# First pair of a gated MLP kernel: x loaded, cast and transposed in pieces of 256 tokens by half of K, products ordered by halves of K

## Chip, cores, metric

One core of a Trainium2 chip. The metric is the device time of one execution in microseconds (us), the lower the better. "The profile" is the hardware profile of one execution. Engines: TensorE (PE in the profile), VectorE (DVE), ScalarE (ACT), GpSimd (POOL); SP is the sequencer that issues most transfers.

## The reference

```python
# x (8, 1024, 1024) -> 8192 tokens x K = 1024; w_gate, w_up (1024, 4096); w_down (4096, 1024), all float32
gate = x @ w_gate
up   = x @ w_up
gate = 0.5 * gate * (1 + np.tanh(np.sqrt(2 / np.pi) * (gate + 0.044715 * gate ** 3)))
return (gate * up) @ w_down
```

## The kernel before

The kernel works in eight passes of 1024 tokens, in float16 with fast matrix multiplication schemes. In the first pass, gate and up are made in 16 "pairs" of 256 columns of each weight. All pairs but the first use a Strassen-like scheme: sums of blocks of x and of the weights go in. The first pair is special: its inputs come straight from memory in float32, before anything else can run, so it uses plain products and is written by hand. It loads x (two halves of 512 tokens, `mh`), casts it on VectorE, transposes it on TensorE into PSUM (the memory that TensorE's results go to; the kernel uses eight banks of it), copies it out, and multiplies. `kh` is the half of K, `w` is gate or up, `j` one of two blocks of 128 columns, `MQ` = 256 tokens, `MH` = 512.

```python
    def x0_load(mh, g):                      # 128 tokens, all of K: rows of 4 KB
        r0 = mh * MH + g * P
        nc.sync.dma_start(out=x0_f32[mh][:, g], in_=x2[r0 : r0 + P, :])
    def x0_cast(mh, g):
        nc.vector.tensor_scalar(x0_f16[:, mh * G + g], x0_f32[mh][:, g], XSC, None, MUL)
    def x0_transpose(mh, g, b):              # 8 transposes into PSUM bank b, two copies out
        ...
    # ... in first_pair():
        for g in range(G):
            x0_cast(0, g)
        warm(9)                              # warm-up matmuls of ones
        late = []
        for g in range(G):
            late.append(x0_transpose(0, g, 4 + g))
            warm(2 if g < G - 1 else 3)
        for w in range(2):
            cast_first(w, 0, slice(0, 256))              # ScalarE
        for f in late:
            f()
        for w in range(2):
            cast_first(w, 1, slice(0, 256), nc.vector.tensor_copy)
        for kh in range(2):
            products(0, kh, slice(0, MH))
        # ... second half of tokens: two transposed pieces, 256 tokens of products, two more, the rest
        outputs(0, 0)
        for w in range(2):
            cast_first(w, 0, slice(256, 512))            # the second pair's weights, ScalarE
        nc.gpsimd.tensor_copy(mark, staging0(1, 0)[:, 0, 256:257])   # waits for load 14
        load_raw(0, 1)                                   # then the third and fourth pairs' weights
        ...
        sum_x(1); sum_w(0, 1, 0); sum_w(0, 1, 1); sum_x(2)           # [joined here] sums of the second
        outputs(1, 0); outputs(1, 1)                                 # pair, all on VectorE
        sum_x(3); sum_w(0, 1, 2); sum_w(0, 1, 3); sum_x(4)
    # order of the 16 first loads, 512 KB each: x(0) four, weights four, x(1) four, next weights four
```

In the timelines read here each engine's instructions start in the order in which they are written.

Of the kernel before, what the change touches and what calls it, by code (L numbers as in the profile page):

```python
# [10 lines left out]
FP16 = mybir.dt.float16  # L11
ADD = mybir.AluOpType.add
SUB = mybir.AluOpType.subtract
MUL = mybir.AluOpType.mult
# [5 lines left out]
XSC = 1.0 / 16.0  # L20
# [153 lines left out]
def kernel(  # L174
# [8 lines left out]
    nc = tc.nc  # L183
    x2 = x.flatten_outer_dims()
    out2 = out.flatten_outer_dims()
    P = 128
# [4 lines left out]
    MH = 512  # L191
    MQ = 256
    HH = H // 2
    KH = K // P // 2
# [3 lines left out]
    G = MH // P  # L198
# [20 lines left out]
    identity = const.tile([P, P], FP16, name="identity")  # L219
# [3 lines left out]
    xq = {  # L223
        n: const.tile([P, KH, MH], FP16, name=f"x_{n}") for n in ("b11", "b12", "b21", "b22")
    }
# [13 lines left out]
    ps_all = psum.tile([P, 8, MH], FP32, name="ps")  # L239
# [5 lines left out]
    ps_free = deque(range(8))  # L245
# [16 lines left out]
    def sum_x(n):  # L262
        o, a, b = {
            1: ("t1", "b12", "b11"), 2: ("t2", "b22", "t1"),
            3: ("t3", "b22", "b12"), 4: ("t4", "b21", "t2"),
        }[n]
        nc.vector.tensor_tensor(xq[o], xq[a], xq[b], SUB)
# [8 lines left out]
    def combine(o, op, a, b):  # L276
# [9 lines left out]
    x0_f32 = {  # L286
        mh: hf[n].bitcast(FP32).rearrange("p (t k) -> p t k", t=G)
        for mh, n in ((0, "a11"), (1, "a21"))
    }
    x0_f16 = hf["a12"].rearrange("p (t a) -> p t a", t=2 * G)  # L290

    def x0_load(mh, g):
        r0 = mh * MH + g * P
        nc.sync.dma_start(out=x0_f32[mh][:, g], in_=x2[r0 : r0 + P, :])

    def x0_cast(mh, g):
        nc.vector.tensor_scalar(x0_f16[:, mh * G + g], x0_f32[mh][:, g], XSC, None, MUL)

    def x0_transpose(mh, g, b):
        h = x0_f16[:, mh * G + g]  # L300
        ps = ps_all[:, b].bitcast(FP16).rearrange("p (k m) -> p k m", m=P)
        for k in range(2 * KH):
            nc.tensor.transpose(ps[:, k], h[:, k * P : (k + 1) * P], identity)
        c = slice(g * P, (g + 1) * P)
        nc.vector.tensor_copy(xq["b11" if mh == 0 else "b12"][:, :, c], ps[:, 0:KH])
        if mh:
            nc.scalar.copy(xq["b22"][:, :, c], ps[:, KH : 2 * KH])
        else:
            return lambda: nc.scalar.copy(xq["b21"][:, :, c], ps[:, KH : 2 * KH])


    def raw(p, q):
        o = 8192 * ((q + p) % 2)
        return rg[:, o : o + 8192].rearrange("p (w k n) -> p w k n", w=2, k=2 * KH)
# [6 lines left out]
    def staging0(w, kh):  # L321
        f = hf["a22"] if kh else xc[:, 8192:16384]
        return f[:, w * 4096 : (w + 1) * 4096].bitcast(FP32).rearrange("p (k n) -> p k n", k=KH)

    def load_first(w, kh, cols):
        nc.sync.dma_start(
            out=staging0(w, kh)[:, :, cols], in_=w_v[w][:, kh * KH : (kh + 1) * KH, cols]
        )

    def cast_first(w, kh, cols, copy=nc.scalar.copy):  # L330
        copy(raw(0, 0)[:, w, kh * KH : (kh + 1) * KH, cols], staging0(w, kh)[:, :, cols])

    def load_raw(p, q):
        if q < NQ:
            for w in range(2):
                nc.gpsimd.dma_start(
                    out=raw(p, q)[:, w], in_=w_v[w][:, :, q * 512 : (q + 1) * 512]
                )

    def sum_w(p, i, k):  # L340
        if i >= NP:
            return
        r, s = raw(p, i // 2), ssum(i)
        e = (i % 2) * 2 * P
        a11, a12 = r[:, :, 0:KH, e : e + P], r[:, :, KH : 2 * KH, e : e + P]
        a21, a22 = r[:, :, 0:KH, e + P : e + 2 * P], r[:, :, KH : 2 * KH, e + P : e + 2 * P]
        o, a, b, op = (
            (s[:, 0], a21, a22, ADD), (s[:, 1], s[:, 0], a11, SUB),
            (s[:, 2], a11, a21, SUB), (s[:, 3], a12, s[:, 1], SUB),
        )[k]  # L350
        nc.vector.tensor_tensor(o, a, b, op)  # L351
# [328 lines left out]
    def gate_up_one(p):  # L680
# [9 lines left out]
        for i in range(NP):  # L690
# [6 lines left out]
            if p == 0 and i == 0:  # L697
                first_pair()
                continue
# [490 lines left out]

    def first_pair():
        bank = {(mh, j, w): 4 * mh + 2 * j + w for mh in range(2) for j in range(2) for w in range(2)}

        def products(mh, kh, c):
            for w in range(2):
                for j in range(2):
                    for k in range(KH):
                        nc.tensor.matmul(
                            ps_all[:, bank[mh, j, w], c],
                            raw(0, 0)[:, w, kh * KH + k, j * P : (j + 1) * P],  # L1200
                            xq[f"b{kh + 1}{mh + 1}"][:, k, c],
                            start=(kh == 0 and k == 0 and c.start == 0),
                            stop=(kh == 1 and k == KH - 1),
                            skip_group_check=True,
                        )

        def outputs(mh, j):
            t = tmp_free.popleft()
            g, u = bank[mh, j, 0], bank[mh, j, 1]
            nc.scalar.activation(tmp[:, t], ps_all[:, g], GELU, scale=GSC)  # L1210
            nc.vector.tensor_tensor(
                hq[f"a{mh + 1}{j + 1}"][:, 0, :], ps_all[:, u], tmp[:, t], MUL
            )
            tmp_free.append(t)

        def warm(n):

            for _ in range(n):
                nc.tensor.matmul(ps_all[:, 0], warm_w, warm_x, start=True, stop=True)

        warm_w, warm_x = hf["s3"][:, 0:P], hf["s3"][:, P : P + MH]
        nc.vector.memset(hf["s3"][:, 0 : P + MH], 1.0)
        nc.scalar.activation(mark, hf["s3"][:, 0:1], GELU)
        for g in range(G):
            x0_cast(0, g)
        warm(9)
        late = []
        for g in range(G):
            late.append(x0_transpose(0, g, 4 + g))
            warm(2 if g < G - 1 else 3)  # L1230

        for w in range(2):
            cast_first(w, 0, slice(0, 256))
        for f in late:
            f()
        for w in range(2):
            cast_first(w, 1, slice(0, 256), nc.vector.tensor_copy)
        for kh in range(2):
            products(0, kh, slice(0, MH))
        for g in range(2):  # L1240
            x0_cast(1, g)
        for g in range(2):
            x0_transpose(1, g, 6 + g)
        for g in range(2, G):
            x0_cast(1, g)
        outputs(0, 0)
        for w in range(2):
            cast_first(w, 0, slice(256, 512))

        nc.gpsimd.tensor_copy(mark, staging0(1, 0)[:, 0, 256:257])  # L1250
        load_raw(0, 1)
        for kh in range(2):
            products(1, kh, slice(0, MQ))
        for g in range(2, G):
            x0_transpose(1, g, g - 2)
        outputs(0, 1)
        for w in range(2):
            cast_first(w, 1, slice(256, 512))
        for kh in range(2):
            products(1, kh, slice(MQ, MH))  # L1260

        ps_free.clear()
        ps_free.extend((0, 2, 1, 3, 4, 5, 6, 7))
        sum_x(1)
        sum_w(0, 1, 0)
        sum_w(0, 1, 1)
        sum_x(2)
        outputs(1, 0)
        outputs(1, 1)
        sum_x(3)  # L1270
        sum_w(0, 1, 2)
        sum_w(0, 1, 3)
        sum_x(4)

    for g in range(G):
        x0_load(0, g)
    for c in (slice(0, 256), slice(256, 512)):
        for kh in range(2):
            for w in range(2):
                load_first(w, kh, c)  # L1280
        if c.start == 0:
            for g in range(G):
                x0_load(1, g)
    for p in range(NPASS):
        if p < FAST:
            gate_up_one(p)
# [36 lines left out]
```

## Time and profile before

| | before |
|---|---|
| time, median of the first 6 executions | 2256.32 us (2255.86 to 2257.22) |
| profiled execution: span | 2254.4 us |
| first product of real data | 11.47 us |
| first matmul of the second pair | 28.72 us |
| TensorE waits after 26 us, whole execution | one, 0.4 us, at 279.69 us |

The lines that carry this are in the prediction. A timeline line is: start, length, engine, source line, operation, output<-input, shape, count; in brackets, the idle time before it and what ended it. A line of the waits is: who waited for whom, then us in total, times, longest. A line of the chain is: start, length, what. In these the shown length of a matmul group has a tail of about 0.17 us.

### The profile page before, as it was taken

The page shows a single profiled execution, that of the slowest core. Times are in us where ns is not written, and L with a number is a line of the kernel's source. Part 1 is how long each engine was busy: PE and PEld are TensorE (multiplying, and loading weights), DVE is VectorE, ACT ScalarE, POOL GpSimd, SP SyncE. Part 2 cuts the span into 40 slices and gives each one's busy share as a digit, 9 for nine tenths or more (in the row PEclk, how much of TensorE's full clock was granted, in tenths as well). Part 3 has the DMA queues.
Part 4 walks back from the last instruction along what each step waited for, and adds up shares of the span by engine and source line. Part 5 has one row for each costly group of instructions (what it writes and reads, how often), then busy time and mean ns, then how long its engine had stood idle before and what let it go on. Part 6 is the DMA issues. An engine that isn't in the chain of part 4 may idle for free.

```text
span 2254.4 us, 42805 instructions
## 1 busy us (share of the span) xinstructions
PE 2246.1 (100%) x16634; PEld 1625.6 (72%) x16634; DVE 1561.7 (69%) x2190; ACT 956.1 (42%) x1866; POOL 679.3 (30%) x825
## 2 busy tenths in 40 slices
PE   9999999999999999999999999999999999999999
PEld 4444444444444445888888888888888888888888
DVE  6576458883588755777776677666786667866674
ACT  4444135651355622666125550356404653055520
POOL 1332013330133200555014550255403543044520
PEclk9999999999999999999999999999999999999999
DMA  9898969989999999999998999989999889988876
GB/s 241 163 207 218 284 184 241 263 264 283 255 227 249 282 309 349 328 342 370 302 339 274 317 304 318 322 270 324 311 324 316 285 308 326 311 311 277 289 285 225
DMA packets 308093, 642.46 MB, mean 285 GB/s; under 512 B 79088, under 2 KB 185328, under 8 KB 287344
## 3 DMA queue, kind: packets, MB, share of 16 engines
q1 hardware_dynamic: 253104, 566.57, 73.2%
q0 software_dynamic: 54784, 73.14, 19.3%
q8 instruction: 130, 2.13, 0.4%
q14 instruction: 75, 0.61, 0.1%
HBM read 574.36 MB, written 138.41 MB: 316 GB/s over the span
## 4 chain that ended last, share of the span: by engine, by line
PE 87%; DMA 2%; SPq 0%; DVE 0%; issue 0%; DVEq 0%
PE ps L848 40%; PE ps L1099 20%; PE ps L626 17%; PE ps L991 10%; DMA wd_quads<-x_sums 1%; SPq L255 0%; DMA ring<-wd_ops 0%; DVE x_sums L452 0%; DVE h_a L923 0%; DVE tmp L1168 0%; DVE x_sums L278 0%; SPq L487 0%; DVEq L278 0%; SPq L535 0%
## 5 line engine op out<-in xcount | busy, mean ns | idle before, releaser
L848 PEld LDWEIGHTS <-ring 128*128 128x128 f16 x8320 | 814.1, 98 | 94.4
L825 POOL TENSOR_TENSOR h_a<-tmp 128x256 f16<-128x256 f32 x640 | 469.3, 753 | 839.3 <-ACT tmp L813 831.9
L848 PE MATMUL ps<-x_sums,ring 128*128 128x256 f16 x5760 | 655.8, 273 | 0.0
L810 DVE TENSOR_TENSOR tmp<-tmp,ps 128x512 f32<-128x512 f32 x640 | 414.5, 683 | 148.1 <-PE ps L848 99.7
L626 PEld LDWEIGHTS <-ring 128*128 128x128 f16 x2632 | 257.5, 98 | 310.4
L795 ACT COPY tmp<-ps 128x512 f32<-128x512 f32 x520 | 304.1, 585 | 237.5 <-PE ps L848 162.8
L626 PE MATMUL ps<-x_sums,ring 128*128 128x512 f16 x1504 | 339.8, 379 | 0.0
L813 ACT ACTIVATE tmp<-tmp 128x256 f32<-128x256 f32 x640 | 264.1, 418 | 172.8 <-DVE tmp L808 79.4
L848 PE MATMUL ps<-x_b,ring 128*128 128x256 f16 x2560 | 305.6, 273 | 0.0
L808 DVE TENSOR_TENSOR tmp<-ps,tmp 128x512 f32<-128x512 f32 x240 | 165.4, 689 | 145.2 <-ACT tmp L795 101.0
L626 PE MATMUL ps<-x_b,ring 128*128 128x512 f16 x1128 | 259.1, 379 | 0.0
L652 POOL TENSOR_TENSOR h_a<-tmp 128x512 f16<-128x512 f32 x94 | 144.5, 1537 | 374.8 <-ACT tmp L650 271.9
L1099 PEld LDWEIGHTS <-h_a 128*128 128x128 f16 x2240 | 219.2, 98 | 25.4
L991 PE MATMUL ps<-ring,h_a 128*128 128x512 f16 x1024 | 222.3, 379 | 0.4 <-DMA ring<-wd_ops 0.4
L1099 PE MATMUL ps<-ring,h_a 128*128 128x256 f16 x1920 | 216.1, 273 | 0.0
L991 PEld LDWEIGHTS <-h_a 128*128 128x128 f16 x1152 | 112.7, 98 | 136.6 <-DMA ring<-wd_ops 0.9
L645 DVE TENSOR_TENSOR tmp<-ps,tmp 128x512 f32<-128x512 f32 x188 | 127.2, 683 | 112.6 <-ACT tmp L637 111.1
L1156 ACT ACTIVATE tmp<-ps 128x512 f32<-128x512 f32 x60 | 35.3, 597 | 362.6 <-PE ps L1099 274.6
L1168 DVE SCALAR_TENSOR_TENSOR tmp<-ps,tmp 128x512 f32<-128x512 f32 x120 | 81.1, 690 | 97.5 <-PE ps L1099 66.6
L351 DVE TENSOR_TENSOR ring<-ring 128x1024 f16<-128x1024 f16 x188 | 138.7, 751 | 11.1 <-DMA ring<-in_w_up_dram 6.9
L637 ACT COPY tmp<-ps 128x512 f32<-128x512 f32 x188 | 109.9, 586 | 77.8 <-PE ps L626 77.8
L1099 PE MATMUL ps<-ring,x_sums 128*128 128x256 f16 x1120 | 126.3, 273 | 0.0
(102 smaller groups left out, 1532.0 us busy)
## 6 DMA issues: line engine op xcount, KB each, us to landing
ring<-w_ops SPq DMA_DIRECT2D x480, 512.0 KB, 5.0
ring<-wd_quads SPq DMA_DIRECT2D x110, 1024.0 KB, 7.0
ring<-wd_ops SPq DMA_DIRECT2D x35, 1024.0 KB, 8.2
out_dram<-tmp SPq DMA_DIRECT2D x128, 256.0 KB, 6.6
w_ops<-h_s SPq DMA_DIRECT2D x128, 256.0 KB, 6.7
ring<-in_w_gate_dram POOLq DMA_DIRECT2D x23, 1024.0 KB, 10.5
ring<-in_w_up_dram POOLq DMA_DIRECT2D x23, 1024.0 KB, 17.8
wd_quads<-x_sums SPq DMA_DIRECT2D x131, 128.0 KB, 6.4
```

What stands on the lines that cost most here:

```text
L351: nc.vector.tensor_tensor(o, a, b, op)
L626: nc.tensor.matmul(ps(b, w), lhs[:, k], rhs[:, k, :], start=(first and k == 0), stop=(k == KH - 1), skip_group_check=True,)
L645: nc.vector.tensor_tensor(o, ps("b", w), o, ADD)
L652: nc.gpsimd.tensor_tensor(hq[TO[n]][:, i, :], tmp[:, t[n, 1]], tmp[:, t[n, 0]], MUL)
L795: nc.scalar.copy(tmp[:, t[o[1]]], ps_all[:, bank[o[2]]])
L808: nc.vector.tensor_tensor(d, b, a, SUB)
L810: nc.vector.tensor_tensor(d, a, b, ADD if o[4] == "add" else SUB)
L813: nc.scalar.activation(d, d, GELU, scale=GSC)
L825: nc.gpsimd.tensor_tensor(h, tmp[:, t[o[1]], MQ : 2 * MQ], g, MUL)
L848: nc.tensor.matmul(ps_all[:, bank[c], w * MQ : (w + 1) * MQ], lhs[:, w, k], rhs[:, k], start=(first and w == 0 and k == 0), stop=(k == KH ...
L991: nc.tensor.matmul(ps_all[:, bank[b, g]], lhs[:, j, g * P : (g + 1) * P], dc[:, n, :], start=(first and j == 0), stop=(j == NP - 1), skip_ ...
L1099: nc.tensor.matmul(ps_all[:, bank[c], m * MQ : (m + 1) * MQ], lhs[:, j, m * P : (m + 1) * P], rhs[:, j, :], start=(first and j == 0 and m ...
```

## The change

The intent: start the products sooner. The first product needs only half of K of x and one weight piece, 1.5 MB instead of 2.5. So x comes in pieces of 256 tokens by half of K, the products run over the first half of K for all tokens, and what belongs to the second half of K follows.

```diff
-    def x0_load(mh, g):
-        r0 = mh * MH + g * P
-        nc.sync.dma_start(out=x0_f32[mh][:, g], in_=x2[r0 : r0 + P, :])
+    def x0_load(mh, gp, kh):
+        r0 = mh * MH + gp * MQ
+        nc.sync.dma_start(
+            out=x0_piece(x0_f32[mh], gp, kh),
+            in_=x2[r0 : r0 + MQ, kh * KH * P : (kh + 1) * KH * P].rearrange("(t p) k -> p t k", p=P),
+        )
 ... (x0_cast likewise)
+    def x0_transpose(mh, gp, kh, b, first=nc.vector.tensor_copy):
 ...
+        first(o[:, 0:2], ps[:, 0:2])
+        nc.scalar.copy(o[:, 2:4], ps[:, 2:4])
 ... first_pair():
+        warm(7)
+        for gp in range(2):
+            x0_cast(0, gp, 0)
+        x0_transpose(0, 0, 0, 4, nc.scalar.copy)
+        warm(2)
+        x0_transpose(0, 1, 0, 5)
+        warm(2)
+        cast_first(0, 0, c0, dve, two[0])
+        cast_first(0, 0, c0, nc.scalar.copy, two[1])
+        cast_first(1, 0, c0, dve)
+        product(0, 0, 0, 0)
 ... (three more products; pieces (1,0,0), (1,1,0), (0,0,1), (0,1,1), each cast, transposed, copied)
+        cast_first(1, 1, c0, dve)
+        product(0, 1, 1, 0)
+        x0_cast(1, 0, 1)
+        x0_transpose(1, 0, 1, 7)
+        outputs(0, 0)
+        product(0, 1, 1, 1)
+        for j in range(2):
+            product(1, 1, 0, j, lo)
+        x0_cast(1, 1, 1)
+        x0_transpose(1, 1, 1, 7)
+        outputs(0, 1)
         for w in range(2):
-            cast_first(w, 0, slice(256, 512))
+            cast_first(w, 0, c1)
 ... (mark, load_raw as before; the remaining products)
+        cast_first(0, 1, c1)
+        cast_first(1, 1, c1, dve)
 ... (the sums and outputs(1, ...) as before)
-    for g in range(G):
-        x0_load(0, g)
+    for kh in range(2):
+        for gp in range(2):
+            x0_load(0, gp, kh)
+        for w in range(2):
+            load_first(w, kh, slice(0, 256))
+        for gp in range(2):
+            x0_load(1, gp, kh)
 ... (then the second pair's four weight pieces, as before)
```

More of the change, by code (lines that the diff above doesn't have):

```diff
@@ L290, with x0_piece, x0_cast @@
     x0_f16 = hf["a12"].rearrange("p (t a) -> p t a", t=2 * G)
-    def x0_load(mh, g):
-        r0 = mh * MH + g * P
-        nc.sync.dma_start(out=x0_f32[mh][:, g], in_=x2[r0 : r0 + P, :])
-    def x0_cast(mh, g):
-        nc.vector.tensor_scalar(x0_f16[:, mh * G + g], x0_f32[mh][:, g], XSC, None, MUL)
-    def x0_transpose(mh, g, b):
-        h = x0_f16[:, mh * G + g]
-        ps = ps_all[:, b].bitcast(FP16).rearrange("p (k m) -> p k m", m=P)
-        for k in range(2 * KH):
-            nc.tensor.transpose(ps[:, k], h[:, k * P : (k + 1) * P], identity)
-        c = slice(g * P, (g + 1) * P)
-        nc.vector.tensor_copy(xq["b11" if mh == 0 else "b12"][:, :, c], ps[:, 0:KH])
-        if mh:
-            nc.scalar.copy(xq["b22"][:, :, c], ps[:, KH : 2 * KH])
-        else:
-            return lambda: nc.scalar.copy(xq["b21"][:, :, c], ps[:, KH : 2 * KH])
+    def x0_piece(t, gp, kh):
+        return t[:, 2 * gp : 2 * gp + 2, kh * KH * P : (kh + 1) * KH * P]
+    def x0_load(mh, gp, kh):
[4 more added lines that the diff above has]
+        )
+    def x0_cast(mh, gp, kh):
+        nc.vector.tensor_scalar(
+            x0_piece(x0_f16, 2 * mh + gp, kh), x0_piece(x0_f32[mh], gp, kh), XSC, None, MUL
+        )
+    def x0_transpose(mh, gp, kh, b, first=nc.vector.tensor_copy):
+        h = x0_piece(x0_f16, 2 * mh + gp, kh)
+        ps = ps_all[:, b].bitcast(FP16).rearrange("p (k m) -> p k m", m=MQ)
+        o = xq[f"b{kh + 1}{mh + 1}"][:, :, gp * MQ : (gp + 1) * MQ]
+        for k in range(KH):
+            for t in range(2):
+                nc.tensor.transpose(
+                    ps[:, k, t * P : (t + 1) * P], h[:, t, k * P : (k + 1) * P], identity
+                )
+        first(o[:, 0:2], ps[:, 0:2])
+        nc.scalar.copy(o[:, 2:4], ps[:, 2:4])
     def raw(p, q):
@@ L328, in load_first, with cast_first @@
         )
-    def cast_first(w, kh, cols, copy=nc.scalar.copy):
-        copy(raw(0, 0)[:, w, kh * KH : (kh + 1) * KH, cols], staging0(w, kh)[:, :, cols])
+    def cast_first(w, kh, cols, copy=nc.scalar.copy, ks=slice(0, KH)):
+        o = raw(0, 0)[:, w, kh * KH : (kh + 1) * KH, cols]
+        copy(o[:, ks], staging0(w, kh)[:, ks, cols])
     def load_raw(p, q):
@@ L1192, in first_pair, with product @@
         bank = {(mh, j, w): 4 * mh + 2 * j + w for mh in range(2) for j in range(2) for w in range(2)}
-        def products(mh, kh, c):
-            for w in range(2):
-                for j in range(2):
-                    for k in range(KH):
-                        nc.tensor.matmul(
-                            ps_all[:, bank[mh, j, w], c],
-                            raw(0, 0)[:, w, kh * KH + k, j * P : (j + 1) * P],
-                            xq[f"b{kh + 1}{mh + 1}"][:, k, c],
-                            start=(kh == 0 and k == 0 and c.start == 0),
-                            stop=(kh == 1 and k == KH - 1),
-                            skip_group_check=True,
-                        )
+        full, lo, hi = slice(0, MH), slice(0, MQ), slice(MQ, MH)
+        def product(mh, kh, w, j, c=full):
+            for k in range(KH):
+                nc.tensor.matmul(
+                    ps_all[:, bank[mh, j, w], c],
+                    raw(0, 0)[:, w, kh * KH + k, j * P : (j + 1) * P],
+                    xq[f"b{kh + 1}{mh + 1}"][:, k, c],
+                    start=(kh == 0 and k == 0 and c.start == 0),
+                    stop=(kh == 1 and k == KH - 1),
+                    skip_group_check=True,
+                )
         def outputs(mh, j):
@@ L1223, in first_pair @@
         nc.scalar.activation(mark, hf["s3"][:, 0:1], GELU)
-        for g in range(G):
-            x0_cast(0, g)
-        warm(9)
-        late = []
-        for g in range(G):
-            late.append(x0_transpose(0, g, 4 + g))
-            warm(2 if g < G - 1 else 3)
-        for w in range(2):
-            cast_first(w, 0, slice(0, 256))
-        for f in late:
-            f()
-        for w in range(2):
-            cast_first(w, 1, slice(0, 256), nc.vector.tensor_copy)
-        for kh in range(2):
-            products(0, kh, slice(0, MH))
@@ L1240, in first_pair @@
-        for g in range(2):
-            x0_cast(1, g)
-        for g in range(2):
-            x0_transpose(1, g, 6 + g)
-        for g in range(2, G):
-            x0_cast(1, g)
-        outputs(0, 0)
-        for w in range(2):
-            cast_first(w, 0, slice(256, 512))
+        two, dve = (slice(0, 2), slice(2, 4)), nc.vector.tensor_copy
+        c0, c1 = slice(0, 256), slice(256, 512)
+        warm(7)
+        for gp in range(2):
+            x0_cast(0, gp, 0)
+        x0_transpose(0, 0, 0, 4, nc.scalar.copy)
@@ new lines, in first_pair @@
+        warm(2)
[5 more added lines that the diff above has]
+        product(0, 0, 0, 0)
+        product(0, 0, 0, 1)
+        product(0, 0, 1, 0)
+        x0_cast(1, 0, 0)
+        x0_transpose(1, 0, 0, 6, nc.scalar.copy)
+        product(0, 0, 1, 1)
+        x0_cast(1, 1, 0)
+        x0_transpose(1, 1, 0, 7)
+        product(1, 0, 0, 0, lo)
+        product(1, 0, 0, 0, hi)
@@ new lines, in first_pair @@
+        x0_cast(0, 0, 1)
+        x0_transpose(0, 0, 1, 7)
+        product(1, 0, 0, 1)
+        x0_cast(0, 1, 1)
+        x0_transpose(0, 1, 1, 7)
+        product(1, 0, 1, 0)
+        cast_first(0, 1, c0, dve, two[0])
+        cast_first(0, 1, c0, nc.scalar.copy, two[1])
+        product(0, 1, 0, 0)
+        product(0, 1, 0, 1)
+        cast_first(1, 1, c0, dve)
[4 more added lines that the diff above has]
+        product(0, 1, 1, 1)
@@ L1250, in first_pair @@
+        for j in range(2):
[3 more added lines that the diff above has]
+        outputs(0, 1)
+        for w in range(2):
+            cast_first(w, 0, c1)
         nc.gpsimd.tensor_copy(mark, staging0(1, 0)[:, 0, 256:257])
         load_raw(0, 1)
+        product(1, 1, 1, 0, lo)
+        product(1, 1, 0, 0, hi)
+        product(1, 1, 0, 1, hi)
+        product(1, 1, 1, 0, hi)
         for kh in range(2):
-            products(1, kh, slice(0, MQ))
@@ L1254, in first_pair @@
-        for g in range(2, G):
-            x0_transpose(1, g, g - 2)
-        outputs(0, 1)
-        for w in range(2):
-            cast_first(w, 1, slice(256, 512))
-        for kh in range(2):
-            products(1, kh, slice(MQ, MH))
+            product(1, kh, 1, 1)
+        cast_first(0, 1, c1)
+        cast_first(1, 1, c1, dve)
         ps_free.clear()
-        ps_free.extend((0, 2, 1, 3, 4, 5, 6, 7))
+        ps_free.extend(range(8))
         sum_x(1)
@@ L1273, in first_pair @@
         sum_x(4)
-    for g in range(G):
-        x0_load(0, g)
-    for c in (slice(0, 256), slice(256, 512)):
-        for kh in range(2):
-            for w in range(2):
-                load_first(w, kh, c)
-        if c.start == 0:
-            for g in range(G):
-                x0_load(1, g)
+    for kh in range(2):
[5 more added lines that the diff above has]
+            x0_load(1, gp, kh)
+    for kh in range(2):
+        for w in range(2):
+            load_first(w, kh, slice(256, 512))
     for p in range(NPASS):
```

## The prediction

> **What bounds the kernel now.** I read the page's busy shares first, then the chain of work that ended last, then TensorE's waits, and last the timeline of the first 45 us, where the change lies.
>
> From the page, and from the chain in order of time:
>
> ```profile
> PE 2246.1 (100%) x16634; PEld 1625.6 (72%) x16634; DVE 1561.7 (69%) x2190; ACT 956.1 (42%) x1866; POOL 679.3 (30%) x825
> ...
> 271.48 8.17 DMA ring<-wd_ops
> 279.65 0.05 issue
> 279.69 27.80 PE ps L991 x128
> 307.50 193.39 PE ps L626 x896
> ```
>
> TensorE (PE) leaves 2254.4 - 2246.1 = 8.3 us of the span unbusy, and from 279.69 us to the end the chain is matmuls without a break. So the kernel is bound by its matmuls; a change can help only in the unbusy time, in time that is "busy" with less than useful work, or by removing matmuls. All waits of TensorE in the whole execution:
>
> ```profile
> PE ps L1219 <- DVE h_s L1222: 1.6, 1, 1.6
> PE ps L1198 <- DVE x_b L305: 1.1, 2, 0.6
> PE ps L1198 <- ACT ring L331: 0.6, 1, 0.6
> PE ps L991 <- DMA ring<-wd_ops: 0.4, 1, 0.4
> PE ps L303 <- DVE h_a L297: 0.2, 1, 0.2
> ```
>
> All but the 0.4 us stand in the first 26 us. The timeline there (start, length, engine, line):
>
> ```profile
> 11.47 7.23 PE L1198 MATMUL ps<-x_b,ring 128*128 128x512 f16 x32 [0.59 <-ACT ring L331]
> ...
> 27.68 1.22 DVE L267 TENSOR_TENSOR x_sums<-x_b,x_b 128x2048 f16<-128x2048 f16 x1
> 28.62 61.30 PEld L626 LDWEIGHTS <-ring 128*128 128x128 f16 x285
> 28.72 3.63 PE L626 MATMUL ps<-x_b,ring 128*128 128x512 f16 x16
> ...
> 34.96 1.22 DVE L267 TENSOR_TENSOR x_sums<-x_b,x_sums 128x2048 f16<-128x2048 f16 x1
> ```
>
> The first pair's products start at 11.47 us, and the second pair starts at 28.72. Until 11.47 TensorE does transposes and warm-up matmuls of ones, waiting for 2 MB of x and 512 KB of w_gate. The first pair holds 64 products of 512 columns (half of them cut into two of 256); at 7.23/32, less the tail of the last, 0.216 us each, that is 13.8 us. The rest of the 17.25 us are transposes and the 1.1 us of waits. The reader is also to see that VectorE (DVE) works through ten instructions without a gap from 27.68 to 36.18 (four sums of x, four of w, two outputs): the second pair needs those sums.
>
> **What the Trainium skill says.** "DMA: Bandwidth & Descriptors", section "Why small descriptors are slow (HBM only)": each packet has a fixed overhead. The trace agrees: at 15 to 18 us, where only x in 4 KB rows moves, the stretches of 1 us show 401 to 418 GB/s; at 20 to 24 us, weights in 1 KB rows, 343 to 358. The same page, "Why a DMA increments its semaphore by 16 and not by 1": a transfer is split over up to 16 engines and has landed when the last of them is done. That is visible: the first 8.39 MB have almost all moved by 24.8 us (35 and 22 GB/s in the two stretches after 25), yet the sixteenth load, issued at 16.32, takes 11.0 us to land, at 27.3. One straggling engine sets the landings. "TensorE: Matmul & The Clock Gate", "What's actually happening": the array starts at half rate and goes to full rate after about 3.4 us of work. The first nine warm-up matmuls start 0.43 us apart, later ones 0.216, so it agrees in kind.
>
> **The change part by part.**
> 1. Removed: 7 warm-up matmuls (18 to 11) and 16 product instructions (96 to 80, by undoing cuts into 256 columns; the columns are the same). All lie before 28.7 us. The 64 transposes stay.
> 2. Moved: the first product now needs 2 pieces of x (half of K) and one w_gate piece, 1.5 MB instead of 2.5 MB. Before, pieces landed at about 4.0, 5.3, 7.6, 8.9, then w_gate at 10.3. After, the third landing, at about 7.7, is w_gate, its cast is split over two engines (half of 0.69 us against half of 1.05), so products start at about 8.3: 3.2 us earlier.
> 3. From there x keeps arriving through the pair. Landings that I expect (1.5 us a weight piece, 1.36 a piece of x, shifts as before): w_up 9.2, x of the second half of tokens 10.6 and 11.9, the second half of K 13.3 and 14.6, w 16.1 and 17.6, the last x at 19.0 and 20.4. TensorE has 13.8 us of products and six pieces of transposes after 8.3, about 0.53 us each (1.06 us for sixteen), 3.2 us; with about 0.8 us of waits for pieces it ends the pair at 26.1, against 28.72. On TensorE alone the change is worth 2.6 us.
> 4. But what the second pair needs is not earlier. The four weight pieces of its columns are still the loads 13 to 16, behind the same bytes; they landed at 23.0, 24.5, 26.0 and 27.3. Now x moves in 2 KB rows instead of 4 KB. With 0.0472 us a 1 KB packet and 0.160 us a 4 KB one on each engine (estimates from packets counted in those stretches), the line between them gives 0.085 for 2 KB, so 6% more for x: 8 pieces x 1.28 x 0.06 = 0.6 us. The sixteenth lands at about 27.9.
> 5. The last piece's cast moves from ScalarE (ACT) to VectorE and stands there directly before the ten sums. So the sums start at 27.9 + 0.05 + 0.61 (a 0.69 us cast, overlapped by 0.08) = 28.6, against 27.68: later by 0.9 us. The last of the ten ends 8.5 us later, at 37.1, and the second pair's P4 needs it; P4 and P3 are the last four groups of products, 0.863 us each. The second pair ends at 37.15 + 3.45 = 40.6. Before: 28.72 + 14 x 0.863 = 40.80, with P4 starting at 37.35 and its sum ready since 36.18, a slack of 1.17 us.
> 6. Sum: 2.6 us are gained in the first pair, about 2.4 of them are given back as waits in the second, where none were. Net about 0.2 us, up to 1 if the 2 KB rows cost nothing. After that pair matmuls bind as before, and the 48 us chain of stores before the stall at 279.69 starts from TensorE's progress at 210 us, so it moves with it.
>
> **The rivals.**
> - The whole 2.6 us are kept: 2253.7. For: no other wait in TensorE's list outside the start, and VectorE is only 69% busy. Against: the landings and the unbroken run of ten instructions above.
> - The next weights bind instead: the load of the third and fourth pairs' weights is held until load 14 has landed (GpSimd waits 23.3 us for it), issued at 25.2 and 26.3, and VectorE waits for it until 39.16. The third pair's P6 needs two sums of it, with two outputs between them in VectorE's order: ready at about 41.7 before, 42.3 with the shift, where P6 would start at 43.2 in my reckoning. It would cap the gain at 1.1 to 1.7 us: about 2255. Near, but behind the sums.
> - ScalarE binds: its cast of load 15 (ready 26.6, ends 27.7), then two GELUs and two copies of 0.55 us, lets P2 start at 29.5 and caps the gain at about 0.95 us. Also behind the sums, by some 0.6 us.
> - Loss: if x in pieces costs more than 1 us of transfer time, the second pair ends later than before: 2256.6 to 2257.
> - A colder clock: fewer warm-up matmuls and a gap before 8.3 us may leave the first products at 0.43 us. Eight of them cost 1.7 us, which the later wait for the sums hides largely; no change of the estimate.
>
> **Range and chances.** 2256.34 - 0.24 = 2256.1 from the sum; the chance that the transfers are as fast as before weighs a little more than a loss, so 2255.9. The rivals span 2253.7 to 2257, executions of the kernel before 2255.86 to 2256.92; 8 in 10: 2254.5 to 2256.9. The 2% line is 45 us away, and all the time before the first product is 11.5 us: faster 0.01, within 0.98, slower 0.01.
>
> **What would show it right or wrong.** Step 2: the first product of real data at about 8.3 us. Step 3: the second pair's first matmul near 26.1. Step 4: the sixteenth load landing near 27.9, later than 27.3. Step 5: VectorE waiting for that load, its first sum of x at 28.6, and new waits of TensorE for VectorE at the second pair's P5, P6 or P4, of some 2 us in all. Step 6: the third pair starting at about 40.6, and the stall at 279.69 still near 0.4 us. I am wrong if the last load lands at 27 us or before, or if no sum is waited for in the second pair: then the gain is 1 us or more. I am also wrong if the later stall grows by what the start gains.

## The result

The changed kernel took 2257.49 us (median of 6 runs, 2256.59 to 2259.72) against 2256.32 for the kernel before, so 1.2 us more; I had predicted 2255.9 and a range to 2256.9. Ratios here are the mean time of one kernel's runs over that of the other's of the same rounds, so not quite the ratio of the medians that I quote: 1.0005, 95% interval 0.9993 to 1.0018. By that interval the 1.2 us are not clear of the noise. What the profile shows in detail is where the expected gain went.

The changed kernel's profile (span 2255.2 us): the busy shares from the page, then three lines of TensorE's waits.

```profile
PE 2244.5 (100%) x16611; PEld 1622.0 (72%) x16611; DVE 1564.7 (69%) x2191; ACT 954.7 (42%) x1867; POOL 676.9 (30%) x825
```

```profile
PE ps L314 <- DVE h_a L304: 2.1, 3, 1.0
...
PE ps L1001 <- DMA ring<-wd_ops: 0.6, 1, 0.6
PE ps L1207 <- ACT x_b L318: 0.5, 2, 0.2
```

Now the timeline, from the first product to the second pair (L314 transposes, L317 and L318 their copies, L304 casts x, L1207 products, L1219 and L1220 outputs, L341 casts weights, L636 later pairs, L652 copies of the second pair's first results):

```profile
8.34 0.61 PE L1207 MATMUL ps<-x_b,ring 128*128 128x512 f16 x2 [0.42 <-DVE ring L341]
...
21.34 2.18 PE L1207 MATMUL ps<-x_b,ring 128*128 128x512 f16 x12
21.61 0.42 DVE L317 COPY x_b<-ps 128x512 f16<-128x512 f16 x1 [2.01 <-PE ps L314]
22.07 0.58 ACT L318 COPY x_b<-ps 128x512 f16<-128x512 f16 x1 [3.40 <-DVE x_b L317]
22.55 0.60 ACT L1219 ACTIVATE tmp<-ps 128x512 f32<-128x512 f32 x1
...
23.19 0.69 DVE L1220 TENSOR_TENSOR h_a<-ps,tmp 128x512 f16<-128x512 f32 x1 [1.15 <-ACT tmp L1219]
23.80 0.69 DVE L304 TENSOR_SCALAR h_a<-h_a 128x1024 f16<-128x1024 f32 x1
...
24.54 0.62 PE L314 MATMUL ps<-identity,h_a 128*128 128x128 f16 x8 [1.02 <-DVE h_a L304]
...
26.62 1.99 ACT L341 CAST ring<-x_sums 128x1024 f16<-128x1024 f32 x2
...
27.57 0.69 DVE L341 CAST ring<-h_a 128x1024 f16<-128x1024 f32 x1
...
28.51 1.05 ACT L341 CAST ring<-h_a 128x1024 f16<-128x1024 f32 x1
...
29.11 3.87 PE L636 MATMUL ps<-x_b,ring 128*128 128x512 f16 x16
29.45 1.09 ACT L1219 ACTIVATE tmp<-ps 128x512 f32<-128x512 f32 x2
...
30.42 1.18 ACT L652 COPY ps<-ps 128x512 f32<-128x512 f32 x2
```

The reader is to see four things. The products do start 3.1 us sooner. The piece of x that the transposes at 24.54 need had landed at 20.2, but its cast stands on VectorE behind an output's multiplication, that waits for a GELU on ScalarE, that stands behind a copy, and that copy waits for VectorE's copy of the other half of the same bank: one chain through three engines. Then ScalarE does the second pair's weight casts at 26.62 although their weights landed at 23.2 and 24.7: they stand behind outputs. And the second pair begins 0.39 us later than before, not sooner. The size of this loss is less sure than that the gain is gone: with the old front unchanged, the second pair started at 29.00 in the profile of e7 (below), where the loads came up to 0.4 us later than in the profile of the kernel before; the changed front gave 29.11 here and 29.14 in e13.

The gaps of TensorE after 8.34 us, from starts and counts (0.216 us for 512 columns, 0.108 for 256, 0.055 a transpose):

| gap before | us | TensorE waited for |
|---|---|---|
| 9.14 | 0.36 | ScalarE's half of a weight cast, behind a copy |
| 14.36 | 0.65 | VectorE's half of a copy (0.25), then ScalarE's half (0.4) |
| 16.39 | 0.5 | ScalarE's half of a copy, to have bank 7 free |
| 17.92 and 18.73 | 0.6 | the halves of a weight cast |
| 24.54 | 1.5 | ScalarE's half of a copy (0.3, at 22.71), then the cast of x behind the output (1.2) |
| 26.29 | 0.65 | VectorE's half of a copy (0.25), then ScalarE's half (0.4) |
| sum | 4.2 | |

In the chain that ended last the loss goes on:

```profile
31.09 179.73 PE ps L636 x832
210.82 62.03 PE ps L1001 x288
272.85 7.58 DMA ring<-wd_ops
280.42 0.05 issue
280.47 27.80 PE ps L1001 x128
```

The second pair's third group waited until 31.09 for ScalarE's copies, behind its three casts and GELUs. The matmuls around the third pair's start come at 39.72 against 39.10 before: 0.62 us late, 0.39 from the first pair and 0.23 from this wait. At 280 us TensorE waits 0.6 us for a load of w_down instead of 0.4; it resumes 0.78 us later than before, and the span is 0.8 us longer. So the profiled execution shows 0.8 us of the 1.2.

### The profile page after: what moved, and what is told of

It reads as the page before. It is cut to its first block, busy times and chain, and to the rows that moved or that the text cites. A ratio compares the mean times of both kernels' runs of the same rounds, so it can differ in the third digit from the quotient of the medians.

```text
span 2255.2 us, 42762 instructions
## 1 busy us (share of the span) xinstructions
PE 2244.5 (100%) x16611; PEld 1622.0 (72%) x16611; DVE 1564.7 (69%) x2191; ACT 954.7 (42%) x1867; POOL 676.9 (30%) x825
## 4 chain that ended last, share of the span: by engine, by line
PE 99%; DMA 1%; ACT 0%; DVE 0%; issue 0%; SPq 0%; DVEq 0%
PE ps L858 40%; PE ps L636 25%; PE ps L1109 20%; PE ps L1001 13%; DMA ring<-wd_ops 0%; PE ps L1207 0%; DMA h_a<-in_x_dram 0%; ACT ring L341 0%; PE ps L314 0%; ACT x_b L318 0%; DVE x_b L317 0%; ACT tmp L1219 0%; DVE h_a L304 0%; DVE h_a L1220 0%; DVE tmp L1178 0%
## 5 line engine op out<-in xcount | busy, mean ns | idle before, releaser
L636 PEld LDWEIGHTS <-ring 128*128 128x128 f16 x2632 | 257.5, 98 | 310.8 <-issue 0.4
L636 PE MATMUL ps<-x_sums,ring 128*128 128x512 f16 x1504 | 339.8, 379 | 0.0
L636 PE MATMUL ps<-x_b,ring 128*128 128x512 f16 x1128 | 259.3, 379 | 0.1
## 6 DMA issues: line engine op xcount, KB each, us to landing
ring<-in_w_gate_dram POOLq DMA_DIRECT2D x23, 1024.0 KB, 10.4
```

The costliest lines, as they stand in the source:

```text
L636: nc.tensor.matmul(ps(b, w), lhs[:, k], rhs[:, k, :], start=(first and k == 0), stop=(k == KH - 1), skip_group_check=True,)
```

## The experiments

Theory A: the orders of VectorE's and ScalarE's queues cost more than the earlier start gains. Rival B: transfers set the time (2 KB rows of x instead of 4 KB, and the last of the 16 loads). Later came A2, on the wait at 280 us, and C, on TensorE's clock at the start. A call's kernels ran on the same chip and share 9 runs of the kernel before: medians 2256.86 (e1, e3, e4, e5), 2256.61 (e6 to e9), 2256.66 (e10 to e13), 2256.71 (e14 to e16).

### e1: the last cast of x two instructions earlier

```diff
         x0_cast(1, 0, 1)
+        x0_cast(1, 1, 1)
         x0_transpose(1, 0, 1, 7)
         outputs(0, 0)
 ...
-        x0_cast(1, 1, 1)
         x0_transpose(1, 1, 1, 7)
```

> The changed kernel with one line moved: the cast of the last piece of x stands two instructions earlier on VectorE, ahead of the first output's multiplication. Theory A (the order of the queues of VectorE and ScalarE costs what the earlier start gains): TensorE's wait of 1.0 us before the last eight transposes (24.5 us) goes to under 0.3; the second pair's first matmul moves from 29.1 to about 27.9; ScalarE's three casts of weights end about 1 us sooner, so the second pair's wait before its third group ends near 30.0 instead of 31.1 and everything behind it, the end too, is about 1.0 us earlier than in the changed kernel: about 0.2 us better than the kernel before. Rival B (the transfers set it: the sixteenth load lands at 27.5 and the sums behind it hold the second pair): the third pair starts where it does in the changed kernel, and the time is the same.

Measured: 2256.40 us (2255.98 to 2257.19), ratio to the kernel before 0.9998 (0.9985 to 1.0012), where the changed kernel has 1.0005. Its timeline:

```profile
23.54 0.61 PE L314 MATMUL ps<-identity,h_a 128*128 128x128 f16 x8
...
27.49 0.69 DVE L341 CAST ring<-h_a 128x1024 f16<-128x1024 f32 x1 [1.04 <-DMA h_a<-in_w_up_dram]
...
28.09 3.87 PE L636 MATMUL ps<-x_b,ring 128*128 128x512 f16 x16
...
29.40 1.19 ACT L652 COPY ps<-ps 128x512 f32<-128x512 f32 x2
```

The wait is gone, the second pair starts 1.02 us earlier than in the changed kernel, and the third group comes at 30.07 instead of 31.09. At the second pair one line's place was worth what A said, and B falls as the main cause there: the loads are the same. But the wait at 280 us was 1.1 us in this execution, so the span fell only from 2255.2 to 2254.6.

### e3: the kernel before, delayed on purpose

```diff
         for kh in range(2):
             products(1, kh, slice(MQ, MH))
+        warm(10)
```

> The kernel before, with ten dummy matmuls (0.216 us each) between the first and the second pair: how much of a delay at the start arrives at the end? If the end follows TensorE (theory A and the prediction's step 6): second pair 2.1 us later, 2.1 us more at the end, the stall near 280 us still near 0.4 us. If something on its own clock (transfers, the chain of stores before 280 us) absorbs it: less than 1.7 us more, and the stall near 280 us gone.

Measured: 2258.18 us (2257.03 to 2259.26), 1.3 us over the kernel before. In the profiled execution (the slowest, 2259.26) the second pair started at 31.12, 2.4 us later than before, and the stretch after the wait at 280 us 3.1 us later than before; the end too. The wait itself was 1.1 us. (2.4 and the 0.7 that this wait was longer make the 3.1.) By the median, less than 1.7 arrived. This run is inconclusive: the profile shows the delay passed on in full, the median does not, and the kernel before itself spread over 2.5 us.

### e4: the front of the changed kernel without its gaps

e1, and both halves of each split weight cast on VectorE, and `outputs(0, 0)` after the last transposes.

```diff
-        cast_first(0, 0, c0, nc.scalar.copy, two[1])
+        cast_first(0, 0, c0, dve, two[1])
 ... (the same for the second half of K)
         x0_transpose(1, 1, 1, 7)
+        outputs(0, 0)
         outputs(0, 1)
```

> The changed kernel with the cast moved up as before, both halves of each split weight cast on VectorE, and the first output after the last transposes. Theory A: TensorE's waits inside the first pair shrink from about 4.0 us to about 1.5, the second pair's first matmul comes at about 26.7, but its third group still waits for ScalarE (copies behind three casts and four GELUs) until about 30.0, so the end is no earlier than with the cast alone: about 1.0 us under the changed kernel, and a new wait of 1.5 to 2.5 us stands in the second pair. If TensorE's own progress in the first pair were what sets the end: 2.4 us under the changed kernel. Rival B (transfers): the same time as the changed kernel.

Measured: 2257.74 us (2256.88 to 2258.39), ratio 1.0004, where about 1.0 us under the changed kernel was expected. The wait at 280 us was 1.6 us in the profiled execution. The second pair started at 28.09, not at 26.7: in this execution TensorE's array was at half rate until past 9 us (the first transposes took 1.03 us instead of 0.62) and the first product came at 9.15. The new wait is there, though smaller than expected, as the pair started later than expected:

```profile
29.88 1.11 ACT L652 COPY ps<-ps 128x512 f32<-128x512 f32 x2
30.56 1.89 PE L636 MATMUL ps<-x_b,ring 128*128 128x512 f16 x8 [0.58 <-ACT ps L652]
```

With smaller gaps at the front (about 2.4 us after the first product instead of 4.2), ScalarE's queue holds the second pair longer. I took this for half a miss, and for the first sign of theory C.

### e5: the queues of VectorE and ScalarE reordered

Same loads as the changed kernel. One engine copies a transposed piece whole, ScalarE casts the next weights where they land, two sums of x come before the last weight casts, and products are cut so that TensorE has work while a piece is copied.

```diff
-        first(o[:, 0:2], ps[:, 0:2])
-        nc.scalar.copy(o[:, 2:4], ps[:, 2:4])
+        first(o[:, 0:2], ps[:, 0:2])
+        second(o[:, 2:4], ps[:, 2:4])        # VectorE too, from the fourth piece on
 ...
+        for w, j in three: product(1, 0, w, j, lo)
+        x0_cast(0, 0, 1)
+        x0_transpose(0, 0, 1, 7, second=dve, after=lambda: x0_cast(0, 1, 1))
+        for w, j in three: product(1, 0, w, j, hi)
 ...
-        for w in range(2):
-            cast_first(w, 0, c1)             # behind outputs
+        cast_first(0, 0, c1)                 # ScalarE, a GELU between the two
+        cast_first(1, 0, c1)
+        sum_x(1); sum_x(2)                   # VectorE, ahead of:
+        cast_first(0, 1, c1, dve)
+        cast_first(1, 1, c1, dve)
+        sum_w(0, 1, 0); sum_w(0, 1, 1)       # then outputs and the other sums in turn
```

> Same loads, same work as the changed kernel; VectorE's and ScalarE's queues reordered throughout: whole transposed pieces copied by one engine, ScalarE's weight casts as soon as the weights land, the first two sums of x ahead of the last weight casts, outputs of the second half of tokens later. Theory A: second pair's first matmul at about 26.3, no wait over 0.5 us for ScalarE or VectorE in it but one for the last weight cast (its fourth group not before 28.2), the third pair then waits for the next weights (landing about 39.3, as in the changed kernel) and starts 1.3 us earlier than in the kernel before: 1.3 us under the kernel before, 2.0 to 2.5 under the changed one. Rival B (2 KB rows and transfers are the loss): not faster than the kernel before.

Measured: 2254.96 us (2254.19 to 2255.84), 1.9 us under the kernel before, ratio 0.9991 (0.9979 to 1.0004). Its timeline:

```profile
26.78 3.62 PE L638 MATMUL ps<-x_b,ring 128*128 128x512 f16 x16
...
39.61 0.69 DVE L363 TENSOR_TENSOR ring<-ring 128x1024 f16<-128x1024 f16 x1 [2.69 <-DMA ring<-in_w_up_dram]
...
40.96 1.02 PE L638 MATMUL ps<-x_sums,ring 128*128 128x512 f16 x4 [0.20 <-DVE h_a L675]
...
42.16 3.19 PE L638 MATMUL ps<-x_sums,ring 128*128 128x512 f16 x14 [0.18 <-DVE ring L363]
```

The second pair starts at 26.78, near what TensorE alone could do, with the same loads: this settles A against B for the first pair. For the time as a whole the interval still includes 1. And the next bound shows, as a rival of the prediction had it: VectorE waits 2.7 us for the third pair's weights. There was no wait at 280 us in this execution.

### e6: the next weights sooner

```diff
-        nc.gpsimd.tensor_copy(mark, staging0(1, 0)[:, 0, 256:257])
+        nc.gpsimd.tensor_copy(mark, staging0(0, 0)[:, 0, 256:257])
```

> The reordered kernel, with the load of the third and fourth pairs' weights let go when load 13 has landed (23.2 us) instead of load 14 (24.9). If these weights are what holds the third pair of the reordered kernel (VectorE waited 2.7 us for them, until 39.6): they land about 1.6 us earlier, at about 38.0, the third pair's group with the second sum starts at about 40.6 instead of 42.2, and the end is 1.3 to 1.6 us earlier, less what a wait at 280 us takes back (0 to 1.6): 2253.4 to 2254.5. If the earlier start only makes them share bandwidth with loads 15 and 16: these land later than 27.9 and nothing is gained.

Measured: 2254.03 us (2253.80 to 2255.72), ratio 0.9991. The sum that waited until 39.61 now starts at 37.72; the third pair's groups that need sums run from 40.55 without those waits; load 16 was not hurt (issued at 17.10, 10.4 us to land, so at 27.5, as in e5). The start is as expected. A wait at 280 us of 0.4 us took part of the gain; a cold start (first product at 9.17) did not, as the second pair came at 26.73, no later than in e5.

### e7 and e8: the wait at 280 us removed, from the kernel before and from the changed one

```diff
-                    if nb == 0 and g == 0 and p + 1 < NPASS:
+                    if nb == (p == 0) and g == 0 and p + 1 < NPASS:     # the transposing loads one chunk later
```

> The kernel before, with the four transposing loads of the next pass's x issued after the load of one chunk of w_down instead of before it (they held that load in the queue for about 10 us, and TensorE waited for it at 280 us: 0.4 us in the kernel before, 0.6, 1.1, 1.6 and 1.1 us in the changed kernel, the moved cast, the front variant and the delay). Theory A2 (that wait is a second, varying loss that has nothing to do with the first pair): the wait at 280 us vanishes, the time falls by 0.4 to 1.2 us, and the five times spread less than the kernel before's. Rival: the loads behind it come late instead and another wait of TensorE shows in the same stage, no gain.

SP's queue in the kernel before, then in e7:

```profile
261.17 10.21 SPq L255 DMA_TRANSPOSE x_b<-x_half  x4
271.48 0.53 SPq L535 DMA_DIRECT2D ring<-wd_ops  x1
```

```profile
261.62 0.39 SPq L535 DMA_DIRECT2D ring<-wd_ops  x1
262.06 13.81 SPq L255 DMA_TRANSPOSE x_b<-x_half  x4
```

Measured: 2255.57 us (2255.53 to 2256.19) against 2256.61 (2255.38 to 2257.51): 1.0 us less by the medians, and a spread of 0.7 us in five runs instead of 2.1 in nine. No wait of TensorE is left after 30 us in its profile. So this wait is a second, varying loss of either kernel, and it blurs comparisons of tenths; A2 holds. The profile's share of it was only 0.4.

> The changed kernel with the same single move in the transfer queue. Theory A (loss at the start of 0.6 us, from the second pair, plus a varying wait at 280 us): no wait at 280 us; the third pair 0.6 us later than in the kernel before, as in the changed kernel; the time 0.6 us (0.4 to 0.8) over the kernel before with the same move, in the profile exactly so. If the changed start had also made the later wait, or other later losses, systematically: more than 1 us over it. Rival B: no difference between the two left.

Measured: 2257.34 us (2256.45 to 2257.64), 1.8 us over e7, not 0.6. No wait at 280 us. But the whole first pair was 1.2 us later than in the changed kernel's profile: first product at 9.20, second pair at 30.29. The loads were not later (load 14 was seen at 24.68). The start shows why:

```profile
5.60 1.04 PE L314 MATMUL ps<-identity,h_a 128*128 128x128 f16 x8 [0.84 <-DVE h_a L304]
```

In the changed kernel's profile the same eight transposes took 0.62 us. The array was still at half rate. This was theory C, the rival that the prediction had dismissed.

### e9: e6 and the move of e7

> The previous one together with the move in the transfer queue. If the two gains are independent (theories A and A2): third pair as in the previous run, no wait at 280 us, 2.8 us (2.2 to 3.4) under the kernel before with the move alone, and 3.3 to 4.0 under the kernel before.

Measured: 2253.76 us (2253.40 to 2254.21), ratio 0.9988 (0.9975 to 1.0000); 1.8 us under e7 and 2.85 under the kernel before. Both are short of the ranges expected (2.2 to 3.4 and 3.3 to 4.0): by the medians e6 gained 2.6 us and e7 1.0, so the gains did not add in full. Why is not shown.

### e13, e10, e12: seven or nine warm-up matmuls

e13 is e8 once more. e10 is e8 with `warm(9)`; e12 is e7 with `warm(7)`.

> The same kernel as e8 (the changed kernel without the wait at 280 us), once more. Theory C (the clock: with 7 warm-up matmuls TensorE's array is at full rate from 5.5 us in some executions and only from about 9.5 us in others; the profiles of the changed kernel, the moved cast and two others show the first, those of e4, e6 and e8 the second): the times fall into two groups about 1.0 us apart, near 2256.4 and 2257.4, and the profile shows one of two starts, first product at 8.3 to 8.5 and second pair at 29.1 to 29.3, or 9.2 and 30.3. Rival (one spread, from transfers): no gap between the times, first product anywhere from 8.3 to 9.2.

> The same with the two warm-up matmuls put back that the change took out of the first group (9 instead of 7). Theory C: the array is at full rate by about 7.5 us in every execution, as in both profiles with nine (the kernel before: second transposes half at full rate at 7.1); first product at 8.4 to 8.9, second pair at 29.2 to 29.7, times in one group within 0.5 us, median 0.5 to 1.0 us under the kernel with seven of the same job. Rival: no difference from it.

> The kernel before (without the wait at 280 us) with 7 warm-up matmuls in the first group instead of 9. Theory C and the slack of the old order: even a cold array until 9.5 us finishes the 32 transposes before w_gate is cast at 11.4, so the first product stays at 11.5 to 11.9 and the time within 0.3 us of the 2255.57 measured with nine. If fewer warm-up matmuls cost time in any order: 0.5 to 1 us more.

| | warm-ups in the first group | median us | range | first product, second pair |
|---|---|---|---|---|
| e13 | 7 | 2257.10 | 2256.39 to 2257.54 | 8.38, 29.14 |
| e10 | 9 | 2256.53 | 2256.40 to 2257.51 | 8.65, 29.41 |
| e12 (old order) | 7 | 2256.08 | 2255.63 to 2256.41 | second pair 29.21 |

e13 was a partial miss: its times do not fall into two clean groups, and its profiled execution (2257.10) had a warm start and another wait of 0.7 us, for an output in the third down stage (862.5 us). e10 went the way of C, with one of five times high (2257.51). That one was profiled: its start was warm, and it lost 0.95 us in three short waits for VectorE and ScalarE between 415 and 446 us, so a high time is not by itself a cold start. In e12 the fewer warm-ups cost 0.5 us against e7 by medians of different calls, more than the 0.3 that I allowed, and its first product came at 12.10, past the 11.9 that I allowed; but its array was at full rate by 7 us and its later second pair (29.21 against 29.00) came with later loads; I can't tell what made that.

### e14, e15, e16: the cold start forced

e14 is e8 with `warm(3)`, e15 is e10 again, e16 is the changed kernel with `warm(9)` and nothing else.

> The changed kernel with the move in the transfer queue (as e8), with 3 warm-up matmuls in the first group instead of 7, so that the array is cold at 5.5 us in every execution. Theory C: first product at 9.2 or a little later, second pair at 30.3 to 31, no execution under 2257.0, median 0.8 to 1.3 us over the kernel with nine of the same job. Rival (the array's clock at the start does not reach the end, as the prediction had it: later waits hide it): the same time as with nine.

> The same kernel as e10 (nine), again, beside the one with three. Theory C: full rate from 5.5 to 7.5 us, first product at 8.3 to 8.7, second pair at 29.1 to 29.5, most times at 2256.4 to 2256.6, none of a group near 2257.4.

> The changed kernel with nine warm-up matmuls and nothing else. Theory C with the losses of theory A left in (0.6 us at the third pair, a varying wait at 280 us): 2256.6 to 2257.2, that is 0.3 to 1.0 us under the changed kernel's 2257.49 and still not under the kernel before. Rival (the clock does not matter): 2257.5.

TensorE in e14, then in e15:

```profile
7.12 1.06 PE L314 MATMUL ps<-identity,h_a 128*128 128x128 f16 x8
...
9.04 0.60 PE L1207 MATMUL ps<-x_b,ring 128*128 128x512 f16 x2 [0.19 <-DVE ring L341]
```

```profile
6.99 0.62 PE L314 MATMUL ps<-identity,h_a 128*128 128x128 f16 x8
...
8.46 0.60 PE L1207 MATMUL ps<-x_b,ring 128*128 128x512 f16 x2 [0.42 <-DVE ring L341]
```

e14 took 2257.43 us (2256.85 to 2257.67), e15 2256.39 (2256.14 to 2256.74), on the same chip: 1.0 us, and the ranges don't meet. So a cold start in the changed order does reach the end. Two details missed: e14's fastest time was under the 2257.0 expected, and its second pair came at 29.80, not from 30.3. In the profiles 0.6 us of the loss shows at the third pair (40.41 against 39.84); e14's profiled execution was its fastest. e16 took 2257.10 (2256.54 to 2258.24), ratio 1.0003: inside what was expected, but its times spread so much (1.7 us) that this run by itself proves nothing.

### e11: all together

e9 with `warm(9)`.

> The reordered kernel with the earlier weights, the move in the transfer queue and nine warm-up matmuls. Theories A, A2 and C: the fastest of all, 2253.3 to 2253.8, 3 us (2.4 to 3.4) under the kernel before; second pair at 26.5 to 26.8. The clock should matter less here than in the changed kernel, as its second pair waits for the last weights (landing at 27.5) in any case: no more than 0.4 us from the same kernel with seven (2253.76).

Measured: 2253.62 us (2253.44 to 2254.07), 3.0 us under the kernel before, ratio 0.9986 (0.9973 to 0.9998): the only interval that excludes 1, and the fastest kernel of all. All of TensorE's waits in it:

```profile
PE ps L1230 <- DVE h_s L1233: 1.6, 1, 1.6
PE ps L314 <- DVE h_a L304: 0.7, 2, 0.4
PE ps L1209 <- DVE ring L343: 0.4, 1, 0.4
```

After the first pair none is left. The nine warm-ups gave 0.14 us over e9, within the spread, as expected.

## Why the prediction was wrong

- What bounds the kernel: right. The gain was to be a few us of the start, and the class "within 2%" was.
- Step 1 counted removed warm-up matmuls as harmless. That was the smaller error; see the last rival.
- Step 2, right: first product at 8.34 us, predicted 8.3.
- Step 3 is the step that failed. It had "about 0.8 us of waits for pieces" and an end at 26.1. The gaps measured 4.2 us and the pair ended at 29.1 (8.34 + 13.8 + 2.65 of transposes + 4.2; the transposes had been put 0.5 us too high). The term was mis-sized because I added waits for data (landings), which I had nearly right, and left out that each piece passes VectorE, TensorE, VectorE, ScalarE and TensorE again, through queues where weight casts and outputs stand in between. e1 gave back 1.0 us by moving one cast; e5 ended the pair at 26.8 with the same loads.
- Step 4, right in kind, too large in one number. In 9 to 13 us, x in 2 KB rows moved at 383 to 387 GB/s, about 6% under the 4 KB rows, as estimated. Load 16 landed 0.3 us later (27.55 against 27.27), not 0.6.
- Step 5 was right about the cast and wrong about what it would hold. The cast at 27.57 started 0.02 us after load 16 had landed, and the output before it had ended 0.1 us sooner; in e1, where VectorE was free, the view says that it waited 1.04 us for this load. VectorE's ten instructions began at 28.18 (predicted 28.6) and their last ended at 36.8; P4, the last product but one of the second pair (four groups are left when it starts), began at 38.0 (39.72 less two groups) and never waited, since the pair had started 3.0 us later than predicted. So the sums' bound was not reached here, and not refuted; e5 put two of them earlier. What held the second pair was ScalarE, the rival that I had put "behind the sums": its copies came at 30.42, where I had its bound at 29.5, because the first pair was late.
- Step 6: the sum was 0.2 us gained; the profile has 0.62 lost by the third pair, and 0.16 more at 280 us. The prediction's sign of being wrong ("if no sum is waited for") came true, but not with the gain that it attached to it: the late first pair left nothing to wait for. That the wait at 280 us "moves with" TensorE was too simple: it measured 0, 0.4, 0.6, 1.1 and 1.6 us in profiles of kernels with that part unchanged.
- The rival of the colder clock was dismissed with the words "no change of the estimate". e14 against e15: 1.0 us. The reason given for dismissing it, a later wait that hides it, had gone: no wait for data stood between the start and the second pair, only a chain through the engines that shifts whole.

The account: of 1.2 us between the medians, the profiles show 0.8. The rest is not accounted for, and noise alone could make it. Cold starts and the wait at 280 us make losses of this size in some executions: three of the eight profiles with seven warm-ups in the new order (e4, e6, e8) were cold, and in the changed order a cold one costs up to 1 us. How often the changed kernel's own timed runs were cold is not seen in times alone and stays open, as does why the wait at 280 us varies. That e3's delay came only in part through to the median is open too.

## What to carry to other kernels

When data is made to arrive earlier in smaller pieces, draw the path of one piece through every engine's queue, in order, with the instructions that stand between, before adding up landings: here 3.1 us won at the start became 0.4 us lost at the second pair, mostly in the queues, and one moved line gave 1.0 us back there. Place what the next stage needs (weight casts, sums of data already there) where its input lands, not behind the outputs of the stage before. And before measuring tenths of a us, find the wait that varies from run to run and take it out of both kernels: for the kernel before that cut the spread from 2.1 to 0.7 us.

## What the Trainium skill lacked or had wrong

- "TensorE: Matmul & The Clock Gate", "What's actually happening", gives about 3.4 us of sustained work for full rate, with a free-running window. The runs fit that, but it doesn't say what a short gap does to a start that just fails it: in the new order seven warm-up matmuls (3.0 us of work, then 0.8 to 1.0 us idle) gave full rate by 5.5 us in five of eight profiles and not before 9 in three; nine gave it between about 5 and 7.3 us in all four that have nine (e10, e11, e15, e16). Its "Part 4: PE-mode transpose" says that the full clock does not engage for transposes. Here eight transposes of 128x128 took 0.62 us once the array was at full rate and 1.03 to 1.06 before; the trace lists them as matmuls with the identity as an operand and doesn't tell their mode, so whether they are what the page means stays open.
- "DMA: Bandwidth & Descriptors" has no trn2 rates for rows of 1 KB and 2 KB in loads into SBUF (the on-chip memory that the engines read) by hardware-generated descriptors: here 343 to 358 GB/s and 383 to 387, beside 401 to 418 for rows of 4 KB, for which it has one.
- The same page warns of two streams of transposing loads in flight together. For the queue that issues them it gives a time only for small tiles and for transfers inside SBUF: here four of them (512x512, float16, from memory) held SP's queue for 10.2 to 14.3 us, with a load that TensorE needed behind them (0 to 1.6 us of wait).
